# A front by contraction tiles, earlier splits for the last down tiles, and a step sooner at two changes of stage, in a one-core decoder-layer kernel

## The chip, the core and the metric

One core of a Trainium2 chip runs the whole layer in one launch. TensorE (PE) does the matmuls; VectorE (DVE), ScalarE (ACT) and GpSimd (POOL) work beside it, each with its own queue of instructions in order; SyncE (SP) issues most transfers. The metric is device time in microseconds (us) of one execution, the median over runs. One execution was recorded by the hardware profiler; its trace gives start and length of each instruction. Tiles are written partitions x columns.

## What is computed

520 tokens (a prompt of 512 and 8 decoding tokens of one step each), model width 1024, all in float32:

```python
def rmsnorm(x, g):
    return x * lax.rsqrt(jnp.mean(x * x, axis=-1, keepdims=True) + EPS) * g

def swiglu(x, w_gate, w_up, w_down):          # 1024 -> 2816 -> 1024
    return (jax.nn.silu(x @ w_gate) * (x @ w_up)) @ w_down

def layer(x, ...):
    x = x + 0.5 * rmsnorm(swiglu(rmsnorm(x, ffn1_pre_g), ...), ffn1_post_g)
    m, states = token_mixer(rmsnorm(x, mix_pre_g), ...)   # projections by w_in, retention and
    x = x + rmsnorm(m, mix_post_g)                        # gated DeltaNet, gates, w_out
    x = x + 0.5 * rmsnorm(swiglu(rmsnorm(x, ffn2_pre_g), ...), ffn2_post_g)
    return x, states
```

## The kernel before

**Products.** x is kept transposed: 8 contraction tiles (KD = 8) of 128 channels by 520 tokens, the tokens in two halves of 260 (HC). A float32 product is made of three passes in a reduced format (fp32r): each operand is split into hi, a cast on ACT, and lo, the rest, a subtraction on DVE; `passes` then issues hi·xh (L408), hi·xl (L409) and lo·xh (L410), all 128x260, into one bank of PSUM, of which there are 8. Weights are split by `split` (L350 cast `whi`, L351 subtraction `wlo`), x by `split_x` (L505 hi = x times the norm's gain, L506 lo; both in a tile `xhl`). The norm's factor 1/rms is per token and comes later, on what the product gives.

**Units and look-ahead.** The weights are a list of units in order of use (`units`): gate and up tiles 128x1024 of each ffn (`gu1`, `gu2`), down tiles in three pieces (8, 7 and 7 contraction tiles), mixer weights. The first PLAIN = 3 (ffn1) or 4 (ffn2) pairs of gate and up are plain products g and u; later pairs go by seven half-size products in place of eight (`sv` rows, from operands made by `token_factors`), as do most down tiles; the first and the last down tile (d = 0 and d = 7) are plain. `prefetch` loads and splits units up to `ahead` units before use (AHEAD = 2; 8 for the half-size ones), within SPLIT_BUFS = 9 buffers; a raw load goes out with two raw buffers.

**Tasks.** PE's order is the program's. Every few matmuls it calls `tick()`, which prefetches and steps small tasks (generators), each `yield n` waiting n ticks. The table LATER adds ticks to single steps by hand. So what an engine does between two other things is set by the tick in which it was written; an engine's queue then keeps that order.

**Front.** `load_first` loads unit 0 in four pieces of 128 KB, each followed by a 260 KB tile of the first token half of x, and then the second token half. `first_units` does g0 and u0, first for half 0 over all k, u0 after g0, then for half 1; the half-0 results are copied out of PSUM into `early`. POOL squares half 0 of x and sums it, ACT and DVE half 1; `inverse_rms` makes the sums over channels by small matmuls (`ss`, L471), the root on POOL, and spreads the factor over partitions by small matmuls (`rb`, L477), copied out by ACT (L559) and DVE (L557). 9 warm matmuls run before the first product.

**Changes of stage.** `down` makes y tile by tile with a sum of squares `acc`; the last tile, d = 7, is done by halves in `staged`. After each half `post` runs: `sums` (`ss`), `ms` on DVE and the root on POOL, `spread` (`rb`), and then for each k: t = y·rb (DVE, L629), x += t (POOL, L631), and two k later `split_x` of the new x. The next stage's products need these xhl. `post` also forces the split of the next stage's first units into that row. The new sum of squares (`pre_rms`) follows. At the very end `post_last` does the same without a next stage: for token half 1, six of the eight output tiles are added by PE (x by an identity product before, L586, t by another, L604, then a copy by ACT, L605, and a transfer of 130 KB each, L606), two by DVE (L608) with one transfer of 260 KB (L609).

Of the kernel before, what the change touches and what calls it, by code (L numbers as in the profile page):

```python
# [7 lines left out]
F32 = mybir.dt.float32  # L8
# [7 lines left out]
P = 128  # L16
# [19 lines left out]
TURN = 48  # L36
WARM = 9
RAW_BUFS, SPLIT_BUFS, AHEAD = 2, 9, 2
# [3 lines left out]
PLAIN = {1: 3, 2: 4}  # L42
SPLIT_H = (8, 21)


LATER = {
    ("begin", 0): {1: 1},
    ("decode_gdn", 0): {1: 8, 2: 2},
# [17 lines left out]
    ("gdn_head", 7): {0: 3},  # L66
    ("leads", 0): {1: 2},
    ("leads", 1): {0: 3},
    ("post", 0): {1: 2, 2: -1},
# [39 lines left out]
def units():  # L109

    out = []
    for f in (1, 2):
        for m in range(KF):
            if m < PLAIN[f]:
                out += [(f"gu{f}", 2 * m, 0, 8), (f"gu{f}", 2 * m + 1, 0, 8)]
# [55 lines left out]
class Kernel:  # L171
    def __init__(self, ctx, tc, a):
# [32 lines left out]
        self.sums_due = []  # L205
        self.hold_sums = True
        self.rooted = False
# [82 lines left out]

    def begin_pair(self, f, m):
# [8 lines left out]
        self.sums_due.append((self.now + SUM_LAG, g, s3, w[2 * m + 1, :, 0:KH]))  # L300
        self.sums_due.append((self.now + SUM_LAG, g, s1, w[2 * m + 1, :, KH:KD]))
        return s1, s3, a22
# [9 lines left out]
    def prefetch(self, force=False, most=9):  # L312
# [5 lines left out]
        while self.split_next < min(last, len(self.unit_list)):  # L318
            j = self.split_next
            seven = self.cost(j) == 1  # L320
            if self.unit_list[j][0] == "seven" and self.hold_sums and not force:
# [171 lines left out]

    def x_of(self, k, hf):
        return self.x[hf][k // 2][:, k % 2]

# [45 lines left out]

    def inverse_rms(self, acc, r, plus):
        nc = self.nc
# [5 lines left out]
        self.rooted = True  # L550
        self.hold = False
        yield 4
        out = self.wk.tile([P, TOK], F32, tag="rb", name=self.name("rb"), bufs=1)
        for hf, (c0, n) in enumerate(HALVES):
            pb = self.spread(s[:, hf * PIECES : (hf + 1) * PIECES])
            if hf:
                nc.vector.tensor_copy(out[:, c0 : c0 + n], pb)  # L557
            else:
                nc.scalar.copy(out[:, c0 : c0 + n], pb)  # L559
        for hf, (c0, n) in enumerate(HALVES):  # L560
            r[hf] = out[:, c0 : c0 + n]
        self.hold_sums = False

    def post_last(self, pairs, acc, sq, hf, plus):
# [28 lines left out]
        if hf:  # L593
            begin(KD - 2)
        for i in range(half):
# [17 lines left out]
    def post(self, y, acc, hf, gnext, xs, r, plus, plus_next):  # L613
# [4 lines left out]
        self.hold = self.hold_sums = True  # L618
        yield 2
        r2 = yield from self.rstd(acc, 1.0 / D, 3, plus and plus[0:PW, hf * PIECES : (hf + 1) * PIECES])  # L620
        if not hf:
# [4 lines left out]
        for k in range(KD + lag):  # L626
# [56 lines left out]
    def down(self, xin, pieces, gpost, gnext, held, plus=None, plus_next=None, x_from=None, seven=None):  # L683
# [39 lines left out]
        def load_x():  # L723
            self.x = self.x_tiles()
            for hf in range(2):
# [53 lines left out]

    def token_factors(self, xs, gcol, F, f):  # L780

        nc = self.nc
        while len(xs[1]) < KD or not self.rooted:
            yield 0

        for m in range(PLAIN[f], PLAIN[f] + 2):
            self.begun[f, m] = self.begin_pair(f, m)
        tt, stt = nc.vector.tensor_tensor, nc.vector.scalar_tensor_tensor
        for k in range(KH):
# [18 lines left out]
            F["B21"].append(xs[0][k + KH])  # L808
            F["B22"].append(xs[1][k + KH])
            yield 2  # L810

    def product7(self, table, F, name, banks, i):
# [14 lines left out]
    def ffn(self, plain, xs, r, gpre, gpost, gnext, plus, plus_next, x_from):  # L827
# [89 lines left out]

        self.spawn(self.token_factors(xs, gpre, F, 1 if x_from is self.a["xT"] else 2))
        lead = self.first_units(xs, "g", ((0,), (1,)) if x_from is self.a["xT"] else ((0, 1), (2, 3)))

        def leads():
            for j in range(0, len(lead), 2):
                yield from hidden(j // 2, *lead[j : j + 2])

        self.spawn(leads())
        for m in range(len(lead) // 2, plain):
            pg = self.product([(self.next_unit(), range(KD))], xs, "g")
# [57 lines left out]
    def run(self):  # L985
# [6 lines left out]
        nc.sync.dma_start(out=self.vec, in_=a["vec"])  # L992
        self.x = self.x_tiles()
        self.ones = c.tile([P, P], F32, name="ones")
# [5 lines left out]
        for i in range(WARM):  # L1000
            nc.tensor.matmul(ps[:, 0:P], self.ones, self.ones, start=True, stop=True)
        self.load_first()
        for k in range(0, KD, 2):
            nc.sync.dma_start(out=self.x[1][k // 2], in_=a["xT"][:, 1, k : k + 2])
        self.cst = c.tile([P, 3, P], F32, name="cst")
        nc.sync.dma_start(out=self.cst, in_=a["cst"])
        self.ident, self.triu, self.negm = (self.cst[:, i, :] for i in range(3))
        self.gh = c.tile([P, 16], F32, name="gh")
# [4 lines left out]
        xs, r = [[], []], [None, None]  # L1013
        for k in range(0, KD, 2):
            self.split(0, [slice(k, k + 2)])
            xs[0] += [self.split_x(k + z, 0, V_G1PRE) for z in range(2)]
        self.split(1, [slice(k, k + 2) for k in range(0, KD, 2)])
        xs[1] += [self.split_x(k, 1, V_G1PRE) for k in range(KD)]
        self.split(2, [slice(0, KD)])
        self.sq = [self.slot("sq") for _ in range(KD)]  # L1020
        for hf, (sq_eng, add_eng) in enumerate(((nc.gpsimd, nc.gpsimd), (nc.scalar, nc.vector))):
            c0, n = HALVES[hf]
            acc = self.sq[0][:, c0 : c0 + n]
            for k in range(KD):
                self.square(k, hf, sq_eng)
                if k:
                    add_eng.tensor_tensor(acc, acc, self.sq[k][:, c0 : c0 + n], ALU.add)
        self.ahead = AHEAD

        def begin():  # L1030
            yield 14
            yield from self.inverse_rms(self.sq[0], r, plus1)

        self.spawn(begin())
        xs, r = self.ffn(PLAIN[1], xs, r, V_G1PRE, self.gh[:, 0:8], V_MPRE, plus1, None, a["xT"])
# [16 lines left out]

    def load_first(self):

        nc, a = self.nc, self.a
        t = self.raw.tile([P, KD, P], F32, tag="raw", name=self.name("raw"))
        self.loaded[0] = t
        self.raw_next = 1
        for k in range(0, KD, 2):
            ks = slice(k, k + 2)  # L1060
            nc.sync.dma_start(out=t[:, ks], in_=a["gu1"][0, :, ks, :])
            nc.sync.dma_start(out=self.x[0][k // 2], in_=a["xT"][:, 0, k : k + 2])
        self.load_to(0)


    def evac_r(self, out, ps, r, off=0):
# [774 lines left out]
def layouts(i):  # L1841
    f = np.float32
    asc = np.ascontiguousarray
    out = {}
    x = np.concatenate([i["x_prompt"][0], i["x_sample"][:, 0]], 0)
    out["xT"] = asc(x.T.reshape(KD, P, 2, HC).transpose(1, 2, 0, 3))

# [3 lines left out]
    for n in (1, 2):  # L1851
        g, u = col_tiles(i[f"ffn{n}_w_gate"][0]), col_tiles(i[f"ffn{n}_w_up"][0])
        out[f"gu{n}"] = asc(np.stack([g, u], 1).reshape(2 * KF, P, KD, P))
        out[f"dn{n}"] = asc(col_tiles(i[f"ffn{n}_w_down"][0]))
    w = i["w_in"][0]
# [86 lines left out]
```

## Time and profile before

| | |
|---|---|
| median of 3 runs | 1201.34 us (1200.16 to 1201.74) |
| profiled execution | 1200.41 us, its span 1198.6 us, mean granted TensorE clock 0.996 |
| PE busy | 1179.1 us, 98% of the span |
| DVE, ACT, POOL busy | 913.7, 603.1, 273.5 us |
| moved by DMA | 170.90 MB, mean 143 GB/s |

The page gives busy time of each engine, the span in 40 slices, and groups of instructions by line; rows of the timeline are start, length, engine, line, operation, output<-inputs, shape, and in brackets the idle time before with what ended it. A row `PE g L409 <- DVE xhl L506: 4.1, 6, 1.0` says that PE waited 4.1 us in 6 waits, the longest 1.0, for DVE's line 506 to end. A matmul row's length overlaps the next one's start, so the pace of PE is read from starts.

### The profile page before, as it was taken

The numbers are of one execution on the slowest core, as the hardware profiler recorded it, in microseconds if no ns is written. First come the engines' busy times: TensorE is split into PE (matmuls) and PEld (weight loads), VectorE is DVE, ScalarE is ACT, GpSimd is POOL, SyncE is SP. The second block draws the span as 40 slices with busy tenths as digits, with TensorE's granted clock in tenths as the row PEclk, the third lists the DMA queues.
The fourth block names the chain that finished last, engine by engine and source line by source line (L and its number), as shares of the span: only waits on it lengthen the run. The fifth ranks groups of instructions, "written<-read, shape, count | busy, mean of one in ns | idle before, by whom it ended". The sixth has DMA issues, their size and how long they took to land. (4 is left out here: it accounts for less than half of the span.)

```text
span 1198.6 us, 25498 instructions
## 1 busy us (share of the span) xinstructions
PE 1179.1 (98%) x9835; PEld 1165.9 (97%) x9835; DVE 913.7 (76%) x1943; ACT 603.1 (50%) x1391; POOL 273.5 (23%) x492
## 2 busy tenths in 40 slices
PE   8999999999999999999999999999999999999998
PEld 8999999999999999999999999998999999999997
DVE  8988888777557788788677777746888888867554
ACT  6565666543336366323344774334555666644331
POOL 4211111000005148756451101404311111000000
PEclk8999999999999999999999999999999999999999
DMA  5877777132342343331467663242587777332342
GB/s 192 217 198 183 184 182 187 47 115 84 107 164 73 123 145 92 100 95 63 121 185 222 227 202 124 76 156 87 165 232 187 184 189 182 94 95 70 108 151 93
DMA packets 79034, 170.90 MB, mean 143 GB/s; under 512 B 17024, under 2 KB 18720, under 8 KB 78912
## 3 DMA queue, kind: packets, MB, share of 16 engines
q1 hardware_dynamic: 66624, 144.98, 37.6%
q0 software_dynamic: 12288, 24.29, 11.1%
q8 instruction: 77, 1.26, 0.4%
q14 instruction: 45, 0.37, 0.1%
HBM read 157.37 MB, written 11.86 MB: 141 GB/s over the span
## 5 line engine op out<-in xcount | busy, mean ns | idle before, releaser
L408 PE MATMUL p<-xhl,whi 128*128 128x260 f32 x784 | 231.0, 295 | 0.0
L409 PE MATMUL p<-xhl,whi 128*128 128x260 f32 x784 | 222.0, 283 | 1.4 <-DVE xhl L506 1.4
L410 PE MATMUL p<-xhl,wlo 128*128 128x260 f32 x784 | 221.4, 282 | 1.8 <-DVE wlo L351 1.8
L351 DVE TENSOR_TENSOR wlo<-raw,whi 128x1024 fp32r<-128x1024 f32 (+2 forms) x121 | 142.3, 1182 | 51.4 <-ACT whi L350 49.6
L408 PE MATMUL sv<-th,w 128*128 128x260 f32 x592 | 167.6, 283 | 0.5 <-ACT q L881 0.5
L409 PE MATMUL sv<-tl,w 128*128 128x260 f32 x592 | 167.6, 283 | 0.0
L410 PE MATMUL sv<-th,w 128*128 128x260 f32 x592 | 167.1, 282 | 0.0
L409 PEld LDWEIGHTS p<-xhl,whi 128*128 128x128 f32 x784 | 148.1, 189 | 2.0 <-DVE xhl L506 1.8
L410 PEld LDWEIGHTS p<-xhl,wlo 128*128 128x128 f32 x784 | 147.7, 188 | 2.2 <-DVE wlo L351 2.2
L408 PEld LDWEIGHTS p<-xhl,whi 128*128 128x128 f32 x784 | 147.9, 189 | 0.7
L350 ACT CAST whi<-raw 128x1024 fp32r<-128x1024 f32 (+2 forms) x121 | 116.3, 971 | 33.5 <-DMA raw<-dn_in 15.5
L369 DVE TENSOR_TENSOR w<-s,w 128x512 fp32r<-128x512 f32 x148 | 101.7, 689 | 37.9 <-ACT w L368 36.5
L307 POOL DMA_DIRECT2D s<-gu_in x74 | 65.1, 965 | 281.1 <-DMA s<-gu_in 93.6
L410 PE MATMUL dn<-hh,wlo 128*128 128x260 f32 x448 | 126.7, 283 | 1.2 <-DVE wlo L351 1.2
L408 PE MATMUL dn<-hh,whi 128*128 128x260 f32 x448 | 127.2, 284 | 0.1
L409 PE MATMUL dn<-hl,whi 128*128 128x260 f32 x448 | 126.7, 283 | 0.0
L410 PE MATMUL sv<-xhl,w 128*128 128x260 f32 x444 | 125.5, 283 | 0.0
L408 PE MATMUL sv<-xhl,w 128*128 128x260 f32 x444 | 125.5, 283 | 0.0
L409 PE MATMUL sv<-xhl,w 128*128 128x260 f32 x444 | 125.4, 282 | 0.0
L408 PEld LDWEIGHTS sv<-th,w 128*128 128x128 f32 x592 | 111.4, 188 | 0.9 <-ACT q L881 0.7
L410 PEld LDWEIGHTS sv<-th,w 128*128 128x128 f32 x592 | 111.8, 189 | 0.0
L409 PEld LDWEIGHTS sv<-tl,w 128*128 128x128 f32 x592 | 111.5, 188 | 0.0
(406 smaller groups left out, 3269.7 us busy)
## 6 DMA issues: line engine op xcount, KB each, us to landing
raw<-gu_in SPq DMA_DIRECT2D x50, 512.0 KB, 4.1
raw<-win_in SPq DMA_DIRECT2D x49, 512.0 KB, 3.6
s<-gu_in SPq DMA_DIRECT2D x74, 256.0 KB, 5.0
s<-gu_in POOLq DMA_DIRECT2D x74, 256.0 KB, 4.7
raw<-dn_in SPq DMA_DIRECT2D x32, 448.0 KB, 3.3
a<-gu_in SPq DMA_DIRECT2D x37, 256.0 KB, 5.0
x<-x SPq DMA_DIRECT2D x32, 260.0 KB, 5.1
raw<-dn_in SPq DMA_DIRECT2D x16, 512.0 KB, 3.5
```

Of the source, the lines that this page charges most:

```text
L307: self.nc.gpsimd.dma_start(out=out, in_=term, accum_op=ALU.add)
L350: self.nc.scalar.copy(hi[:, ks], t[:, ks])
L351: self.nc.vector.tensor_tensor(lo[:, ks], t[:, ks], hi[:, ks].bitcast(F32), ALU.subtract)
L369: nc.vector.tensor_tensor(w[:, 1], t[i], w[:, 0].bitcast(F32), ALU.subtract)
L408: mm(ps, hi[:, k, :], xh, start=first, stop=False, skip_group_check=more)
L409: mm(ps, hi[:, k, :], xl, start=False, stop=False, skip_group_check=more)
L410: mm(ps, lo[:, k, :], xh, start=False, stop=last, skip_group_check=more)
```

## The change

1. **Front.** The first three units (g0, u0, g1; LEAD = 3) are laid out by contraction tile (`lead`: 128 x 8 x 384) and x as `xk` (128 x 8 x 520), so that one load of 192 KB and one of 260 KB bring all that contraction tile k needs. `front` goes over k: for each, six banks (three units by two halves) get their 18 passes. ACT casts 384 columns of weights, scales 520 of x and squares 520; DVE subtracts twice and adds the squares up. POOL squares nothing any more, and the copies `early` fall away. The six loads of `begin_pairs` (first operands of the seven-product pairs) are issued right behind. WARM is 11. u1 is then done by halves (`staged`), with `ss` ahead of the last 18 passes of the front and `rb` with its two copies within u1.
2. **Last down tiles.** `prefetch` takes two units more of `ahead` for d = 7 of both ffns, so their three pieces are split earlier, and the third one's raw load goes out ahead of the x loads.
3. **Changes of stage** (`post`, first half). `sums` one tick sooner, `spread` one tick less behind; in `rstd` the next split is forced right behind `ms`, and in the row of k only where fewer than two units are split. Before the mixer this puts `ss` 6 matmuls sooner and `rb` 6; before ffn2 `ss` 6 sooner and `rb` 12.
4. **Tail.** Four output tiles by identity products in place of six; DVE adds the other four.

DVE at the front, before: `wlo` in quarters, xhl by halves of tokens (raw, x, vec: weights, activations and gains as loaded).

```order
L351 TENSOR_TENSOR wlo_130<-raw_107,whi_129 128x256
L506 SCALAR_TENSOR_TENSOR xhl_133<-x_85,vec,xhl_133 128x260
L506 SCALAR_TENSOR_TENSOR xhl_136<-x_85,vec,xhl_136 128x260
L351 TENSOR_TENSOR wlo_130<-raw_107,whi_129 128x256
L506 SCALAR_TENSOR_TENSOR xhl_141<-x_86,vec,xhl_141 128x260
L506 SCALAR_TENSOR_TENSOR xhl_144<-x_86,vec,xhl_144 128x260
L351 TENSOR_TENSOR wlo_130<-raw_107,whi_129 128x256
```

The same place now: per contraction tile the three units' lo, x's lo over all tokens, and from the third on the sum of squares.

```order
L1090 TENSOR_TENSOR wl_162<-leadw_101,wl_162 128x384
L1091 SCALAR_TENSOR_TENSOR xl_164<-x_103,vec,xh_163 128x520
L1090 TENSOR_TENSOR wl_169<-leadw_105,wl_169 128x384
L1091 SCALAR_TENSOR_TENSOR xl_171<-x_107,vec,xh_170 128x520
L1090 TENSOR_TENSOR wl_178<-leadw_109,wl_178 128x384
L1091 SCALAR_TENSOR_TENSOR xl_180<-x_111,vec,xh_179 128x520
L1103 TENSOR_TENSOR sq_176<-sq_176,sq_185 128x520
```

Two steps of DVE (a tile's lo of three units and of x) now carry 18 passes of PE; before, three steps (a quarter of `wlo`, two halves of tokens) carried 6. DVE at the end of ffn1, before (`wlo` 896 wide: the two seven-tile pieces of d = 7; `wlo_4821`, 1024: its third piece; `wlo_4827`: the mixer's first unit):

```order
L351 TENSOR_TENSOR wlo_4745<-raw_4467,whi_4744 128x896
L672 TENSOR_TENSOR c_4765<-dn_4750,u_4726 128x260
L653 TENSOR_TENSOR t_4767<-c_4765,dn_4564 128x260
L517 TENSOR_TENSOR acc_643_3486<-acc_643_3486,s_4770 128x260
L710 TENSOR_SCALAR y_4769<-t_4767,gh 128x260
L678 TENSOR_TENSOR v_4788<-q_4763,dn_4668 128x260
L653 TENSOR_TENSOR t_4790<-v_4788,dn_4565 128x260
L517 TENSOR_TENSOR acc_644_3487<-acc_644_3487,s_4792 128x260
L710 TENSOR_SCALAR y_4769<-t_4790,gh 128x260
L351 TENSOR_TENSOR wlo_4797<-raw_4630,whi_4796 128x896
L653 TENSOR_TENSOR t_4814<-u_4786,dn_4470 128x260
```

Now, same place:

```order
L351 TENSOR_TENSOR wlo_4678<-raw_4442,whi_4677 128x896
L351 TENSOR_TENSOR wlo_4726<-raw_4605,whi_4725 128x896
L682 TENSOR_TENSOR c_4746<-dn_4731,u_4707 128x260
L663 TENSOR_TENSOR t_4748<-c_4746,dn_4539 128x260
L523 TENSOR_TENSOR acc_649_3461<-acc_649_3461,s_4751 128x260
L720 TENSOR_SCALAR y_4750<-t_4748,gh 128x260
L351 TENSOR_TENSOR wlo_4756<-raw_4681,whi_4755 128x1024
L688 TENSOR_TENSOR v_4775<-q_4744,dn_4643 128x260
L663 TENSOR_TENSOR t_4777<-v_4775,dn_4540 128x260
```

The second piece stands eight steps sooner, the third ahead of two of the last evacuations instead of behind all. DVE at the change from ffn1 to the mixer, before:

```order
L463 SCALAR_TENSOR_TENSOR ms_4939<-ss_4935,plus_12_127 87x3
L629 TENSOR_TENSOR t_4959<-y_3710,rb_4955 128x260
L629 TENSOR_TENSOR t_4968<-y_3999,rb_4955 128x260
L351 TENSOR_TENSOR wlo_4972<-raw_4824,whi_4971 128x1024
L629 TENSOR_TENSOR t_4983<-y_4055,rb_4955 128x260
L506 SCALAR_TENSOR_TENSOR xhl_4986<-x_4728,vec,xhl_4986 128x260
```

And now:

```order
L463 SCALAR_TENSOR_TENSOR ms_4908<-ss_4904,plus_26_154 87x3
L351 TENSOR_TENSOR wlo_4919<-raw_4759,whi_4918 128x1024
L639 TENSOR_TENSOR t_4934<-y_3685,rb_4930 128x260
L639 TENSOR_TENSOR t_4943<-y_3974,rb_4930 128x260
L639 TENSOR_TENSOR t_4952<-y_4030,rb_4930 128x260
L512 SCALAR_TENSOR_TENSOR xhl_4955<-x_4709,vec,xhl_4955 128x260
```

The split moved out of the row of t. Before ffn2 a split of this kind keeps its place behind the second t.

The diff, cut:

```diff
-WARM = 9
+WARM = 11
+LEAD = 3
 LATER = {
-    ("begin", 0): {1: 1},
+    ("begin", 0): {2: 2},
...
 def prefetch(self, force=False, most=9):
             ahead += j > 0 and not seven and self.unit_list[j - 1][0] == "down7"
+            if self.unit_list[j][0][:2] == "dn" and self.unit_list[j][1] == KD - 1:
+                ahead += 2
...
-    def rstd(self, acc, scale, wait, plus):
+    def rstd(self, acc, scale, wait, plus, split=False):
         ps = self.bank("ss")
         self.sums(ps, acc, PIECES)
         _, r = self.root(ps, PIECES, scale, plus)
+        if split:
+            yield 1
+            self.prefetch(True, 1)
+            wait -= 1
         yield wait
         return self.spread(r)
...
 def post_last(...):
         if hf:
-            begin(KD - 2)
+            begin(KD // 2)
...
-            if hf and i < half - 1:
+            if hf and i < half // 2:
...
 def post(...):
-        yield 2
-        r2 = yield from self.rstd(acc, 1.0 / D, 3, ...)
+        yield 2 if hf else 1
+        r2 = yield from self.rstd(acc, 1.0 / D, 3 if hf else 2, ..., not hf)
...
-            if not hf and k == 1:
+            if not hf and k == 1 and self.split_next < self.use_next + 2:
                 self.prefetch(True, 1)
...
+        self.x, self.x_whole, self.lead_w = None, [], []
+        for k in range(KD):
+            self.lead_w.append(self.slot("leadw", (P, LEAD * P)))
+            nc.sync.dma_start(out=self.lead_w[k], in_=a["lead"][:, k])
+            self.x_whole.append(self.slot("x"))
+            nc.sync.dma_start(out=self.x_whole[k], in_=a["xk"][:, k])
+        self.load_to(0)
...
+    def front(self, xs, r):
...
+        def operands(k):
+            x, raw = self.x_whole[k], self.lead_w[k]
...
+            nc.scalar.copy(w[:, 0], raw)
+            nc.scalar.activation(hi, x, AF.Copy, scale=g)
+            tt(w[:, 1], raw, w[:, 0].bitcast(F32), ALU.subtract)
+            stt(out=lo, in0=x, scalar=g, in1=hi.bitcast(F32), op0=ALU.mult, op1=ALU.subtract)
...
+        for k in range(KD):
+            operands(k)
+            if k:
+                squares(k - 1)
+        squares(KD - 1)
...
+        for k in range(KD):
+            for j in range(LEAD):
+                for hf in range(2):
+                    self.passes(ws[k], j, xs[hf][k], banks[j][hf], k == 0, k == KD - 1)
+                self.tick()
+            self.release(1)
+            if k == KD - 3:
+                self.spawn(begin())
+                self.prefetch(True, 1)
```

More of the change, by code (lines that the diff above doesn't have):

```diff
@@ L112, in units @@
     for f in (1, 2):
-        for m in range(KF):
-            if m < PLAIN[f]:
-                out += [(f"gu{f}", 2 * m, 0, 8), (f"gu{f}", 2 * m + 1, 0, 8)]
+        out += [(f"gu{f}", j, 0, 8) for j in range(LEAD if f == 1 else 0, 2 * PLAIN[f])]
         out += [("seven", f, m, i) for m, i in stream(PLAIN[f])]
@@ L320, in prefetch @@
             seven = self.cost(j) == 1
-            if self.unit_list[j][0] == "seven" and self.hold_sums and not force:
+            if self.unit_list[j][0] == "seven" and (self.hold_sums or j >= self.pairs_upto) and not force:
                 break
@@ L809, in token_factors @@
             F["B22"].append(xs[1][k + KH])
+            if f == 1 and not k:
+                while not self.rooted:
+                    yield 0
+            elif f == 1 and k == 1:
+                while r[1] is None:
+                    yield 0
+                yield 2
+            elif f == 1 and k == KH - 2:
+                self.pairs_upto = 2 * PLAIN[1] - LEAD + 2
             yield 2
+        self.pairs_upto = len(self.unit_list)
     def product7(self, table, F, name, banks, i):
@@ L916, in pair, with up, leads @@
             return banks, at
[L918 to L926, printed above, removed]
+        self.spawn(self.token_factors(xs, r, gpre, F, 1 if x_from is self.a["xT"] else 2))
+        if x_from is self.a["xT"]:
+            lead = self.front(xs, r)
+            self.spawn(hidden(0, *lead[0:2]))
+            half = [None, None]
+            def up(j, hf, ps):
+                half[hf] = ps
+                if hf:
+                    self.spawn(hidden(1, lead[2], half))
+            self.staged([lambda: [(self.next_unit(), range(KD))]], KD, xs, "u", up, False)
+            done = 2
+        else:
+            lead = self.first_units(xs, "g", ((0, 1), (2, 3)))
+            def leads():
+                for j in range(0, len(lead), 2):
+                    yield from hidden(j // 2, *lead[j : j + 2])
+            self.spawn(leads())
+            done = 2
+        for m in range(done, plain):
             pg = self.product([(self.next_unit(), range(KD))], xs, "g")
@@ L1013, in run @@
         xs, r = [[], []], [None, None]
[L1014 to L1034, printed above, removed]
+        self.front_plus = plus1
         xs, r = self.ffn(PLAIN[1], xs, r, V_G1PRE, self.gh[:, 0:8], V_MPRE, plus1, None, a["xT"])
```

90 lines of the change are left out of this document (62 added, 28 removed).

## The prediction, before the run

> **What bounds the kernel now.** I read the page first, then TensorE's waits over the span, then a timeline and a table by stretch for the front, and last the places that the change touches. From the page, span, busy time and clock:
>
> ```profile
> span 1198.6 us, 25498 instructions
> ...
> PE 1179.1 (98%) x9835; PEld 1165.9 (97%) x9835; DVE 913.7 (76%) x1943; ACT 603.1 (50%) x1391; POOL 273.5 (23%) x492
> ...
> PEclk8999999999999999999999999999999999999999
> ```
>
> TensorE (PE) is busy 98% of the span, so only two things can move the time: matmuls that fall away, and time in which PE waits or runs below full clock. The clock is below full in the first slice alone. PE's waits over the whole span:
>
> ```profile
> PE g L409 <- DVE xhl L506: 4.1, 6, 1.0
> PE dn L410 <- DVE wlo L351: 2.0, 4, 0.6
> PE p L410 <- DVE wlo L351: 1.8, 2, 1.4
> PE p L409 <- DVE xhl L506: 1.4, 2, 1.0
> PE g L410 <- DVE wlo L351: 1.1, 2, 0.6
> PE u L408 <- ACT rb L559: 0.5, 1, 0.5
> PE u L408 <- DVE rb L557: 0.4, 1, 0.4
> ```
>
> Columns: total us, times, longest. Most rows lie where the change is made: the front (g on xhl), the two ends of a down stage (dn on wlo), the two changes of stage. The front, PE's rows one by one and then by stretch:
>
> ```profile
> 2.68 2.46 PE L1001 MATMUL warm<-ones 128*128 128x128 f32 x11
> 5.33 0.39 PE L408 MATMUL g<-xhl,whi 128*128 128x260 f32 x1 [0.19 <-ACT xhl L505]
> 6.29 0.39 PE L409 MATMUL g<-xhl,whi 128*128 128x260 f32 x1 [0.57 <-DVE xhl L506]
> 6.52 0.28 PE L410 MATMUL g<-xhl,wlo 128*128 128x260 f32 x1
> ...
> 9.19 0.42 PE L410 MATMUL g<-xhl,wlo 128*128 128x260 f32 x1
> 9.40 0.42 PE L408 MATMUL g<-xhl,whi 128*128 128x260 f32 x1
> ```
>
> ```profile
> 4.92:8.34 3.42, 1.87 (x9) 1.05 (x8) 3.03 (x4) 2.54 (x7) 3.26 (x5) 1.00 0.88 279
> 8.34:18.57 10.23, 8.52 (x33) 7.66 (x34) 10.23 (x16) 8.67 (x23) 7.96 (x11) 0.50 0.65 231
> 18.57:50.56 31.99, 31.99 (x274) 31.99 (x273) 29.87 (x60) 18.34 (x38) 7.06 (x7) 1.00 0.72 199
> 830.94:834.35 3.41, 2.27 (x17) 1.86 (x16) 2.43 (x3) 2.03 (x4) 0.33 (x1) 1.00 0.18 20
> ```
>
> Columns after the length: busy time of PE, weight loads, DVE, ACT, POOL, then granted clock, DMA share, GB/s. PE is starved in the first stretch (1.87 of 3.42 us), the clock then stands at 0.50 for 10.23 us, in which DVE is busy throughout, and only after that does PE run without a break. In the last row, a like thinning at the second change of stage, 2.27 us of work kept the clock. At half clock two starts lie 0.21 us apart (9.19, 9.40); at full clock three passes take 0.36, 0.12 each (next fence), and the row of 50.56 is the first `seven` product, the front's end. A wait costs more than its row says: the 0.57 before 6.29 stands for a start 0.96 after the last and one more of 0.23, 0.95 above two of 0.12. I add 0.3 for each wait below.
>
> ```profile
> 50.20 0.28 PE L408 MATMUL u<-xhl,whi 128*128 128x260 f32 x1
> ...
> 50.56 0.28 PE L408 MATMUL sv<-xhl,w 128*128 128x260 f32 x1
> ```
>
> **The front.** Six plain units of 48 matmuls are 6 x 48 x 0.12 = 34.6 us; the norm's `ss` and `rb`, 24 small ones, add 2.0 (31.99 less the other 250 x 0.12). So 36.6 us of work, which before took 50.56 - 5.33 = 45.2: 8.6 are lost. What the new order loses of that depends on its operands:
>
> ```profile
> 4.77 0.92 ACT L505 ACTIVATE xhl<-x,vec 128x260 fp32r<-128x260 f32 x2 [1.03 <-DMA x<-xT_in]
> ```
>
> ```profile
> 5.31 1.80 DVE L506 SCALAR_TENSOR_TENSOR xhl<-x,vec,xhl 128x260 fp32r<-128x260 f32 x2 [1.11 <-ACT xhl L505]
> ...
> 17.23 2.88 DVE L506 SCALAR_TENSOR_TENSOR xhl<-x,vec,xhl 128x260 fp32r<-128x260 f32 x7
> ```
>
> ```profile
> L351 DVE TENSOR_TENSOR wlo<-raw,whi 128x1024 fp32r<-128x1024 f32 x81 | 101.6, 1259 | 27.3 <-ACT whi L350 27.0
> L804 DVE TENSOR_TENSOR tl<-ta,th 128x520 fp32r<-128x520 f32 x8 | 5.5, 693 | 0.0
> ```
>
> ```profile
> L368 ACT CAST w<-s 128x512 fp32r<-128x512 f32 x148 | 91.3, 618 | 34.8 <-DVE s L364 23.8 <-PE sv L410 7.1 <-DVE s L372 3.4
> ```
>
> Transfers: a contraction tile is 192 + 260 KB, 0.46 MB. At the 279 and 231 GB/s of the first two stretches that is 1.7 to 2.0 us. The first x landed at 4.77 before, behind 128 KB of weights; now 64 KB more are ahead of it, 0.28 us: 5.05. DVE: the squares leave POOL, so the 0.90 us of a 128x260 subtraction (1.80 for two) becomes the 0.41 of the row at 17.23. A tile costs DVE a 384-wide subtraction (0.55, between 0.41 for 260 and 0.69 for 520), one of 520 and one addition of 520 (0.69 each): 1.9 us. ACT has three forms, 384 wide and twice 520, 0.62 at 512: 1.8. PE has 18 x 0.12 = 2.15. So PE is the slowest by a little, and all three hide behind it once it runs.
>
> It starts at 5.05 + 0.62 (ACT) + 0.69 (DVE) + 0.1 for handing over (before, ACT's first half ended at 5.23, PE began at 5.33) = 6.45. The warm rows ended at 5.14; two warm matmuls more, two rows each, end them near 5.6, so the window from 4.92 to 8.34 holds 0.7 us of them and about 16 passes of 0.12, some 2.6 us of work against 1.87: above the 2.27 that kept the clock. I take full clock throughout. Losses left: 6.45 - 5.33 = 1.1 at the start; 0.15 at the second tile (landed at 5.05 + 1.7 to 2.0, operands 1.3 later at 8.1 to 8.4, PE asking at 8.6; 0 to 0.3); 0.5 at u1's first third pass, whose split stands on DVE behind the last sums and the first token factors (8.4 + 6 tiles x 1.9 + a last addition 0.69 + four of 0.41 and two of 0.69 = 23.6, the split's end 1.26 later near 24.9), while PE asks near 24.4 (6.6 + 17.3, `ss`, two passes); 0.5 where `rb` and the second half of u1 take turns for banks that ACT and DVE must copy out (the `u` on `rb` rows, 0.5 and 0.4, are this hand-over in ffn2). Sum 2.2; end near 5.33 + 36.6 + 2.2 = 44.1. **-6.4**. Bounds: -7.5 (only the start lost), -4.7 (one more window at half clock, rival 1). The early `s` and `a` loads on SP stand behind all front loads; nothing of the front queues behind them.
>
> The Trainium skill ("DMA: Bandwidth & Descriptors", Measured) gives 138 GB/s for 64 KB, 341 for 1 MB, and asks for 1 MiB a transfer; reading 200 GB/s between them, an estimate, a tile takes 2.3 us and the front loses some 1.2 more. The stretches above, with transfers of 128 to 512 KB, ran at 231 to 279, so I keep those.
>
> **Last down tiles.** Two more units of lead put each `wlo` of d = 7 ahead of its use by up to two units more (21 matmuls, 2.5 us, each). What waits there now, at the end of ffn1 and of ffn2:
>
> ```profile
> PE dn L410 <- DVE wlo L351: 1.2, 2, 0.6
> ...
> PE dn L410 <- DVE wlo L351: 0.9, 2, 0.6
> ```
>
> 2.1 + 4 x 0.3 = 3.3; the last wait of the four, on a third unit whose load comes last, I count by half: **-3.0**; bounds -2.1 (the rows alone) and -3.5. The third unit's load goes ahead of x on SP; x is needed only after the sums, ten us on. The splits, up to 1.26 us each on DVE, go beside evacuations that PE doesn't wait for.
>
> **First change of stage.** Rows of the chain now (`rb` on PE, t on DVE, the next split's `wlo`, the first x operand):
>
> ```profile
> 363.67 0.80 PE L477 MATMUL rb<-cst,rs 87*128 87x87 f32 x6
> 364.51 0.76 DVE L629 TENSOR_TENSOR t<-y,rb 128x260 f32<-128x260 f32 x2 [2.02 <-PE rb L477]
> 365.19 1.71 DVE L351 TENSOR_TENSOR wlo<-raw,whi 128x1024 fp32r<-128x1024 f32 x1
> 365.85 0.51 ACT L505 ACTIVATE xhl<-x,vec 128x260 fp32r<-128x260 f32 x1 [5.17 <-POOL x L631]
> ```
>
> The first `lo` stands behind that `wlo`, and so does the third t. Now the sums come 6 matmuls sooner (0.72), and `wlo` stands between `ms` and the first t, in time that DVE spent idle ([2.02 <-PE rb]). PE's waits on p after it were 1.4 on xhl (two) and 0.4 on wlo (1.8 less its longest, which lies past 409 us and isn't touched): 2.7 with 0.3 for each. The chain is 0.72 earlier and 1.2 shorter (the 1.71 less what DVE would have waited for POOL in that time, 0.5): **-1.9**; bounds -0.7 (the earlier sums alone) and -2.7. New risk: `ss` comes before the accumulator is summed; it has 24 matmuls, 2.9 us, for ACT's square and DVE's addition, 0.46 + 0.41 by the rows above. Nothing.
>
> **Second change of stage.** Sums and `rb` 12 matmuls (1.44) sooner, but the `wlo` stays between two t:
>
> ```profile
> 819.81 1.66 DVE L351 TENSOR_TENSOR wlo<-raw,whi 128x1024 fp32r<-128x1024 f32 x1
> ```
>
> ```profile
> PE g L410 <- DVE wlo L351: 1.1, 2, 0.6
> PE g L409 <- DVE xhl L506: 1.0, 1, 1.0
> ```
>
> The wait on xhl (1.3 with its 0.3) goes. The two waits on the next splits stay: DVE has no less to do, and three evacuations (0.41 or so each) now stand inside the t row. `ss` follows the evacuation by 12 matmuls (1.4 us) where 0.46 + 0.41 are needed, behind whatever ACT and DVE are at (a 1024-wide split is 1.26): up to 0.7 of wait. **-1.2**; bounds -2.7 (all but one 0.3 of 2.1 + 0.9) and, if the evacuations (3 x 0.41) and that 0.7 exceed the 1.44, +0.5.
>
> **Tail.** Four output tiles by identity products:
>
> ```profile
> 1190.05 1.51 PE L586 MATMUL xo<-x,cst 128*128 128x260 f32 x6
> ...
> 1192.44 2.79 SPq L606 DMA_DIRECT2D yT_out<-x  x6
> ...
> 1195.32 0.40 SPq L609 DMA_DIRECT2D yT_out<-x  x1
> ```
>
> Two of the three x products after `rb` go (1.0 us), so the first t product starts when t is there, 0.45 sooner; SP has six issues of 0.47 in place of seven; DVE's one more addition of 520 (0.69) ends at about the same time. Last issue near 1194.5: **-0.7**; bounds 0 (the bytes decide) and -1.0.
>
> Sum: -6.4 - 3.0 - 1.9 - 1.2 - 0.7 = -13.2, from the profiled execution's 1200.41 to 1187.2. The median of the runs, 1201.34, lies 0.93 above that execution: 1188.1. All parts at their best give 1201.34 - 17.4 = 1183.9, all at their worst 1201.34 - 7.0 = 1194.3.
>
> **Rivals.** (1) One more window of 3.41 us at half clock, from 8.34: PE then does half, +1.7, 1189.8. For it: the clock fell here before; my 2.6 us of work is not far above 2.27, and operands 1 us late would put it below. The trace's fall came after a stretch with PE busy for 1.87 of 3.42 us. The Trainium skill ("TensorE: Matmul & The Clock Gate", Part 1: The HAM clock gate) has the clock fall only after an idle window, and its windows free-running; by that the front would keep its clock, as in my sum. A window more than half busy lost it here, so the trace doesn't bear that rule out; the phase no run here shows. (2) What the stage changes and down tiles gain is handed on: PE arrives sooner at splits that DVE does no sooner (the two `wlo` at the second change, the sums): 2 to 4 us of the 6.1 come back, 1191.1. For it: DVE is busy 76%. Against: waits later in both stages are small. (3) The other side: the front's operands come slower than PE. If a tile took p us instead of 2.15, the front would be 8 x (p - 2.15) longer; 13.2 us are used up at p = 3.8, where PE would also stand at half clock (18 x 0.21 = 3.8 a tile). Above it the kernel is slower: at 4.5, +5.6, 1207. There transfers would run at 0.46 MB / 4.5 us = 100 GB/s, or DVE at twice its rows. Against: 231 and 279. (4) The same at its edge: the front all at half clock, 3.8 a tile (+13.2), with the other gains kept: near 1201.3, no change. Against: 2.27 us of work in a window kept the clock, and DVE has 1.9 a tile.
>
> **How the numbers follow.** Forecast 0.68 (its own range 1185 to 1191), rival 1 0.14, rival 2 0.11, rival 3 0.03, rival 4 0.04. The range 1184.5 to 1192.5 holds the first three but for their edges. A measurement of this kernel tells 0.2%, 2.4 us, from no change: faster 0.93, same 0.04, slower 0.03.
>
> **What would show it.** Clock 1.00 after about 5 us and no 0.50 behind 8.34; the first sv near 44; `dn` on wlo gone from PE's waits; the waits of p on xhl gone, and no wlo between the t's at the first change; g on wlo still there at the second; new `u` on `rb` waits before 45 us; last output issue 0.7 us nearer to `rb`. A half-clock window in the front, or g waiting on transfers at each tile, would make it wrong.

## The result: 8.7 us faster, where 13.2 were forecast

| | before | after |
|---|---|---|
| median | 1201.54 us (4 runs, 1200.16 to 1202.13) | 1192.87 us (4 runs, 1192.46 to 1193.32) |
| profiled execution, its span | 1200.41, 1198.6 us | 1193.21, 1191.4 us |

The ratio is 0.9927, 95% interval 0.9911 to 0.9942. Forecast were 1188.1 and a range from 1184.5 to 1192.5. The page after, and PE's waits over the span (total us, times, longest):

```profile
span 1191.4 us, 25448 instructions
...
PE 1174.1 (99%) x9831; PEld 1163.2 (98%) x9831; DVE 907.3 (76%) x1935; ACT 602.9 (51%) x1378; POOL 262.4 (22%) x477
```

```profile
PE rb L477 <- POOL rs L465: 1.8, 3, 0.9
PE pV L1687 <- DVE pack L1679: 1.8, 2, 1.4
PE sv L408 <- ACT q L905: 1.8, 2, 1.2
PE p L410 <- DVE wlo L351: 1.4, 1, 1.4
```

The 4.1 us of g on xhl, the 2.0 of dn on wlo and the 1.4 of p on xhl are gone. Three of these four rows are new or larger: `rb` on POOL's root, pV (a step of the mixer's triangular solves) on DVE, and sv on ACT's copy q. The front, by rows and by stretch (length; busy time of PE, weight loads, DVE, ACT, POOL; granted clock; DMA share; GB/s):

```profile
5.90 0.39 PE L408 MATMUL g<-xh,wl 128*128 128x260 f32 x1
6.70 0.39 PE L409 MATMUL g<-xl,wl 128*128 128x260 f32 x1 [0.41 <-DVE xl L1091]
...
44.33 0.28 PE L408 MATMUL sv<-xh,w 128*128 128x260 f32 x1
```

```profile
5.61:9.02 3.41, 3.00 (x23) 2.62 (x22) 2.26 (x4) 2.68 (x6) 0.00 (x0) 1.00 0.98 328
9.02:44.33 35.31, 34.79 (x295) 34.61 (x294) 32.43 (x61) 24.75 (x47) 7.03 (x7) 1.00 0.84 238
640.49:643.90 3.41, 1.98 (x20) 1.73 (x19) 3.09 (x9) 0.64 (x2) 0.00 (x0) 1.00 1.06 328
643.90:647.32 3.42, 3.42 (x18) 3.42 (x17) 2.85 (x8) 1.57 (x9) 0.54 (x1) 0.50 0.96 331
```

The front went as forecast: first sv at 44.33 (forecast 44.1), full clock from 5.61, PE busy 34.79 of 35.31. The last row was not forecast: PE ran at half clock for 3.42 us in the mixer.

To see where time went, I cut each trace at the same matmuls of PE, counted from its first, and took the us between their starts. (With the front of before, four warm rows are fewer, and the count is four lower.) The last columns are kernels of the experiments below.

| stretch (rows of PE in the changed kernel) | before | after | front_only | no_front | after_again | ramp | split_before2 |
|---|---|---|---|---|---|---|---|
| front, to the first sv (334) | 50.56 | 44.33 | 44.71 | 51.06 | 44.49 | 44.14 | 44.56 |
| the next 46 | 5.48 | 7.29 | 7.26 | 5.48 | 7.26 | 5.52 | 7.27 |
| end of ffn1 (2830 to 2890) | 8.94 | 7.20 | 8.67 | 7.18 | 7.20 | 7.20 | 7.20 |
| first change (to 3060) | 23.09 | 22.51 | 23.05 | 22.57 | 22.53 | 22.52 | 21.91 |
| gates (3380 to 3420) | 4.70 | 4.72 | 6.24 | 4.68 | 6.23 | 4.71 | 4.72 |
| a solve (5340 to 5400) | 7.22 | 9.94 | 7.18 | 7.28 | 7.18 | 8.26 | 7.18 |
| second change (6750 to 6900) | 21.50 | 19.36 | 21.47 | 19.37 | 19.36 | 19.35 | 19.36 |
| end of ffn2 (9660 to 9710) | 7.74 | 6.00 | 7.47 | 6.01 | 6.00 | 6.00 | 6.00 |

So of the front's 6.2 us, 1.8 came back within 46 matmuls. The stretches repeat to 0.1 us between kernels that are alike there, but for the gates, the solve and the front's start. After minus before: -6.2 + 1.8 - 1.7 - 0.6 + 2.7 - 2.1 - 1.7 is -7.8; 1.3 more comes on in the long runs of products between, 0.9 of it from row 380 to 2830 (ffn1) and 0.4 in the mixer, and the tail has -0.6: -7.1, against 7.2 by the spans. Of the 0.9, 0.6 can't be put down to the change: no_front has it too, from row 1500 to 2830, where none of its edits acts yet.

### The profile page after: what moved, and what is told of

The parts are those of the page before. It is cut to its first block, busy times and chain, and to the rows that moved or that the text cites. A ratio compares the mean times of both kernels' runs of the same rounds, so it can differ in the third digit from the quotient of the medians.

```text
span 1191.4 us, 25448 instructions
## 1 busy us (share of the span) xinstructions
PE 1174.1 (99%) x9831; PEld 1163.2 (98%) x9831; DVE 907.3 (76%) x1935; ACT 602.9 (51%) x1378; POOL 262.4 (22%) x477
## 5 line engine op out<-in xcount | busy, mean ns | idle before, releaser
L351 DVE TENSOR_TENSOR wlo<-raw,whi 128x1024 fp32r<-128x1024 f32 (+1 forms) x111 | 133.0, 1203 | 50.0 <-ACT whi L350 48.4
L350 ACT CAST whi<-raw 128x1024 fp32r<-128x1024 f32 (+1 forms) x111 | 111.6, 1012 | 31.5 <-DMA raw<-dn_in 16.6
L368 ACT CAST w<-s 128x512 fp32r<-128x512 f32 x148 | 91.4, 618 | 33.8 <-DVE s L364 23.6
L465 POOL TENSOR_TENSOR rs<-ms,mhalf 87x3 f32<-87x3 f32 (+1 forms) x9 | 11.6, 1288 | 372.0 <-DVE ms L463 309.7
L410 PEld LDWEIGHTS dn<-hh,wlo 128*128 128x128 f32 x448 | 84.4, 188 | 0.0
```

Of the source, the lines that this page charges most:

```text
L350: self.nc.scalar.copy(hi[:, ks], t[:, ks])
L351: self.nc.vector.tensor_tensor(lo[:, ks], t[:, ks], hi[:, ks].bitcast(F32), ALU.subtract)
L368: nc.scalar.copy(w[:, 0], t[i])
L410: mm(ps, lo[:, k, :], xh, start=False, stop=last, skip_group_check=more)
L465: self.nc.gpsimd.tensor_tensor(r[0:PW], m[0:PW], self.mhalf[0:PW].to_broadcast([PW, n]), ALU.pow)
```

## The experiments

My theory after the result: the front's gain is handed on to splits behind it (theory 1), the first change loses to POOL's root, and the mixer's loss is an accident of the clock. The rivals are in the expectations.

**Parts alone or undone.** front_only: the first part without the others. no_front: the others without it. no_stage: `rstd`, `post` as before. no_down: without these lines:

```diff
-            if self.unit_list[j][0][:2] == "dn" and self.unit_list[j][1] == KD - 1:
-                ahead += 2
```

front_only:

> The new front alone; down tiles, changes of stage and tail as before. Theory 1 (the front's 6.2 us are partly handed on: PE meets the half-size splits before DVE has made them): first sv near 44.3, then a wait of 1.4 to 1.6 us on ACT's copy q near 49, some 3.6 us kept at the first dn tiles; in the mixer the wait on pack stays near 0.5 as before and the clock full: 3.4 to 4.0 us faster than before. Rival A (the front's own gain is all kept and the loss is due to the other parts): no wait near 49, 6 us faster. Rival B (whenever PE is some 5 us early in the mixer, the pack wait grows to 1.6 us and the clock falls for 3.4 us): as theory 1, but 1 to 1.5 us faster in all.

no_front:

> The front as before, with the earlier splits of the last down tiles, the sooner steps at both changes of stage and the short tail. Theory 1: the trace's differences hold one by one: 1.6 at the end of ffn1, 0.6 at the first change, 2.0 at the second, 1.6 at the end of ffn2, 0.7 in the tail, 6.5 us faster than before, with no loss of clock in the mixer. Rival A (the down and stage gains depend on the early front): below 4 us. Rival B (the pack wait and the lost clock come from the sooner steps, not from the front): 3.8 us, with the half-clock window near 650.

no_stage:

> The changed kernel with both changes of stage as before: sums, spread and the forced split at their old places. Theory 1 (at the first change the split right behind ms runs beside POOL's root and makes it 1.8 us in place of 0.9, and the second sums wait on DVE all the same, so that 0.6 us is all that was gained): root back at 0.9 us, the waits on xhl back to 1.4; the first change costs 0.6 more, the second 2.0 more: 2.6 us slower than the changed kernel unless the mixer's wait moves. Rival (the sooner steps gain what was forecast, 1.9 and 1.2): 3.1 us slower, and root at 0.9 in both.

no_down:

> The changed kernel without the two units more of lead for the last down tiles. Theory 1: waits of dn on wlo come back, two at each end, 1.6 us and 1.6 us: 3.2 us slower than the changed kernel if nothing else moves. Rival (the waits only move to the sums behind them, since DVE has no less to do): 1 us slower or less. The mixer's pack wait is a third reading of its size at another offset of PE: 1.6 again and a half-clock window if it depends on the new front, 0.5 if on PE being 5.5 us early.

Measured, against 1200.8 us of the kernel before on that chip (15 runs; the changed kernel was not run there, so what a part undone costs is read by stretch):

| | median us | ratio, 95% interval |
|---|---|---|
| front_only | 1198.42 | 0.9979, 0.9970 to 0.9988 |
| no_front | 1195.01 | 0.9950, 0.9936 to 0.9963 |
| no_stage | 1195.95 | 0.9957, 0.9944 to 0.9969 |
| no_down | 1194.93 | 0.9950, 0.9938 to 0.9963 |

The new front, worth 6 us at its end, is worth 2.4 in the whole (3.4 to 4.0 expected); the small edits are worth 5.8 (6.5 expected). By stretch the undone parts cost about what the changed kernel's trace had them gain: without the stage edits the first change takes 23.04 and the second 21.51 (0.5 and 2.2 more); without the down edit the two ends take 8.66 and 7.52 (1.5 each, for a gain of 1.7). Rival A of front_only falls: the wait near 49 is there with the front alone, and no_front has the 5.48 of before. The rivals of no_front and no_down fall as well: the small edits keep their gain without the new front, with no loss of clock near 650. My reading of the mixer held by half for front_only: the solve stayed at 7.18, so rival B falls too, but the clock was not full, since a window at half clock came elsewhere, at the gates. Busy time by stretch, and the gates' rows, of front_only:

```profile
415.72:419.13 3.41, 3.41 (x31) 3.36 (x30) 2.17 (x5) 3.41 (x12) 0.19 (x1) 1.00 1.04 391
419.13:422.55 3.42, 3.42 (x18) 3.42 (x17) 2.68 (x7) 2.60 (x14) 3.16 (x4) 0.50 0.59 178
```

```profile
415.83 0.29 PE L1335 MATMUL gc<-gg,cst 128*128 128x16 f32 x2
416.05 1.05 PE L1338 MATMUL gc<-cst,gg 8*128 8x8 f32 x8
416.97 1.03 PE L1338 MATMUL gc<-cst,beta 8*128 8x8 f32 x8
417.93 1.16 PE L1360 MATMUL gbc<-cst,gg 128*128 128x128 f32 x8
```

PE's rows fill the window from 415.72 (3.41 of 3.41), yet the clock fell behind it: 16 of its 31 matmuls were 8 columns wide on 8 partitions.

**The wait near 49.** What stands ahead of it in the changed kernel, on DVE, ACT and PE:

```profile
48.64 0.69 DVE L364 SCALAR_TENSOR_TENSOR s<-s,raw 128x512 f32<-128x512 f32 x1
```

```profile
49.36 0.62 ACT L368 CAST w<-s 128x512 fp32r<-128x512 f32 x1 [2.06 <-DVE s L364]
49.89 0.37 ACT L905 COPY q<-sv 128x260 f32<-128x260 f32 x1
```

```profile
50.31 0.39 PE L408 MATMUL sv<-th,w 128*128 128x260 f32 x1 [1.24 <-ACT q L905]
```

PE waits for a bank that ACT's copy q empties. The copy has long been possible (the last pass of its product starts at 47.09), but ACT first waits 2.06 us with a cast for DVE's sum s, of a unit that is needed some units later, and DVE is still at the splits of units up to 8 ahead. Counted in the traces, ACT had started 5 casts for half-size units by 2.5 us ahead of the first sv before the change, and 2 after it; in the next 5 us it starts 4 before, 7 after. Is it DVE's backlog from the front, or the order? no_sq_adds takes 4.8 us of additions off DVE (its norm is then another one, so it serves for the times alone); ahead5 keeps the work and shortens the look-ahead:

```diff
-            else:
-                tt(acc, acc, sq, ALU.add)
```

```diff
             ahead = 8 if seven and self.ahead else self.ahead
+            if seven and self.use_next < 2 * PLAIN[1] + 8:
+                ahead = 5
```

no_sq_adds:

> The changed kernel without the seven 128x520 additions of squares on DVE in the front (the norm's sum is then of the first contraction tile alone); all else as in the changed kernel. Theory D (DVE's backlog from the front, 4.8 us of it these additions, makes the half-size splits late): u1's wait on wlo is gone, and the 1.4 us before the sv product near 49 fall below 0.3, so 1.3 to 1.6 us faster than the changed kernel, first sv near 44.2 as there. Theory O (the copy q of a bank stands on ACT behind a cast that was split ahead of need, and the order alone makes the wait): the wait stays at 1 us or more.

ahead5:

> The changed kernel with the half-size units split at most 5 units ahead in place of 8 until the second pair of ffn1: the same work on DVE and ACT, in another order; copy q then stands behind no cast that waits for DVE's sum s2. Theory O (order): the wait near 49 falls from 1.4 to below 0.4 and no other of its size comes up in the next 10 us: 1.2 us faster than the changed kernel. Theory D (DVE's backlog): the wait goes over to w on DVE or to the next q, 1 us or more in all, and the time is the changed kernel's within 0.5 us.

no_sq_adds took 1191.64 us (0.9924, 0.9903 to 0.9945, against 1201.08) and has the wait unchanged; ahead5 took 1193.46 (0.9939, 0.9923 to 0.9956) and has it no more there, but has one where the look-ahead jumps from 5 to 8:

```profile
PE sv L408 <- ACT q L905: 1.2, 1, 1.2
```

```profile
68.40 0.36 PE L410 MATMUL sv<-xh,w 128*128 128x260 f32 x1 [1.81 <-ACT w L370]
```

(The first row: PE's waits of no_sq_adds from 44 to 75 us; the second: the timeline of ahead5.) So DVE's total isn't what makes the wait. In ahead5 it went over to the cast of an operand, not far from what theory D allowed, and behind it came a window at half clock (at 69.8), so that rows 380 to 1500 take 3.8 us longer than in after_again. Whether the burst makes the wait, or DVE has too little time in any order, was still open. To tell, ramp lets the look-ahead grow by one for every 14 units:

```diff
+            if seven:
+                ahead = min(ahead, 5 + max(0, self.use_next - 2 * PLAIN[1] + LEAD) // 14)
```

> The changed kernel with the half-size units split 5 ahead at first, and one more for every 14 units used, up to 8. Theory O (a burst of look-ahead splits, in the in-order queues of ACT and DVE, stands before the copies that free PE's banks; at a jump of the look-ahead from 5 to 8 the wait came back, 2.0 us): without a jump the wait near 49 is gone and none over 0.5 us comes before 100; 1.4 us faster than the changed kernel. Theory D (DVE has too little time for these splits in any order): a wait of 1 us or more comes later, no gain.

1190.99 us (0.9917, 0.9901 to 0.9932, against 1201.35). The 46 matmuls take 5.52 us, as before the change, ACT starts 5 of those casts in place of 7, and no wait comes from 44 to 75. Theory O holds by the stretch. By the median against the changed kernel's 1191.79 on the same chip, 0.8 us, it can't be told. Part of the 1.7 us is lost again later: rows 6900 to 8500, in ffn2, take 195.00 in place of after_again's 194.19, as they do in the other two kernels with a shorter look-ahead (195.01 in ahead5, 194.98 in ramp_split); why is open.

**The first change.** POOL's root, what DVE does beside it, and `rb`, in the changed kernel; and the root before:

```profile
356.59 1.81 POOL L465 TENSOR_TENSOR rs<-ms,mhalf 87x3 f32<-87x3 f32 x1 [148.43 <-DVE ms L463]
```

```profile
356.43 1.23 DVE L351 TENSOR_TENSOR wlo<-raw,whi 128x1024 fp32r<-128x1024 f32 x1
```

```profile
358.45 0.34 PE L477 MATMUL rb<-cst,rs 87*128 87x87 f32 x1 [0.59 <-POOL rs L465]
```

```profile
362.57 0.88 POOL L465 TENSOR_TENSOR rs<-ms,mhalf 87x3 f32<-87x3 f32 x1 [157.28 <-DVE ms L463]
```

The same root on 87x3 numbers takes 1.81 us in place of 0.88 when the wide subtraction runs beside it, and PE waits (in no_stage, without the split there, it takes 0.88 again). split_before_sums moved the split ahead of `ms`, but also put `rb` and the rest of `post` a tick sooner; split_before2 keeps all ticks:

```diff
+        if split:
+            self.prefetch(True, 1)
         ps = self.bank("ss")
         self.sums(ps, acc, PIECES)
         _, r = self.root(ps, PIECES, scale, plus)
         if split:
             yield 1
-            self.prefetch(True, 1)
             wait -= 1
```

split_before_sums (the same without `yield 1`):

> The changed kernel with the forced split at the first change of stage ahead of ms on DVE instead of right behind it. Theory R (a wide split on DVE beside POOL's root takes the root from 0.9 to 1.8 us, and rb waits for it): root back at 0.9, ms some 0.4 later, rb's wait at 357.6 from 0.9 to 0.4 or so, 0.4 to 0.5 us faster there. Rival (the root is long for another reason): root stays near 1.8 and rb's wait grows to 1.2. Its mixer tells again whether the pack wait of 1.6 us is there when the stages are sooner.

split_before2:

> The changed kernel with the forced split of the first change of stage ahead of ms on DVE, all other steps at their old ticks. Theory R (a wide split beside POOL's root makes the root 0.9 us longer and rb wait): root 0.9, rb's first wait at most 0.9 as it starts later by the split, x ready 0.5 sooner; the second ms and rb as in the changed kernel (wait 1.1 to 1.2); 0.3 to 0.6 us faster. Rival: the first operands of p aren't what the second ms waits for, so that rb 0.5 sooner only lengthens its wait: no gain within 0.2.

split_before_sums took 1196.52 us (0.9963, 0.9950 to 0.9975): the root was back at 0.88, but the tick put both next splits ahead of the second `ms` on DVE, and `rb` waited there for 3.7 us (first row, PE's waits from 340 to 380). split_before2 took 1190.54 (0.9909, 0.9896 to 0.9923, against 1201.35), with the first of the two waits gone (second row, waits from 354 to 380) and the root at 0.89:

```profile
PE rb L477 <- POOL rs L465: 4.4, 2, 3.7
```

```profile
PE rb L477 <- POOL rs L465: 0.9, 1, 0.9
```

```profile
357.40 0.89 POOL L465 TENSOR_TENSOR rs<-ms,mhalf 87x3 f32<-87x3 f32 x1 [148.99 <-DVE ms L463]
```

The stretch went from 22.5 to 21.91: 0.6 us, and the rival falls. The second wait, 0.9, stays. In the changed kernel `ms` stands there on DVE behind an x operand, and `rb` behind it on PE (before, `rb` didn't wait here):

```profile
368.55 0.49 DVE L512 SCALAR_TENSOR_TENSOR xhl<-x,vec,xhl 128x260 fp32r<-128x260 f32 x1 [0.29 <-ACT xhl L511]
368.96 0.15 DVE L463 SCALAR_TENSOR_TENSOR ms<-ss,plus 87x3 f32<-87x3 f32 x1
```

```profile
370.09 0.34 PE L477 MATMUL rb<-cst,rs 87*128 87x87 f32 x1 [0.92 <-POOL rs L465]
```

In split_before_sums it is this wait that grew.

**The mixer's solve.** solve_later puts the step that waits two ticks later (`yield 4` to `yield 6` ahead of pV64); after_again is the changed kernel once more.

> The changed kernel with the last step but one of each head's triangular solve (pV64) two ticks, 12 matmuls or 1.4 us, later in PE's order. Theory P (PE came 1.2 us too soon for a chain of small transfers, ACT and DVE, and the pause also cost the clock): the wait of 1.6 near 641 falls below 0.4, no half-clock window there, 1.2 to 2.8 us faster than the changed kernel. Rival (the head's chain is what is late, and PE waits at its next step instead): a wait of 1 us at pX or pu behind, and no gain.

> The changed kernel once more, on the chip of the next three. What is open: is the pack wait of 1.7 us at 641 a property of the kernel, or of one execution. If of one execution (it was 0.5 in three kernels that are the same there): 0.5 here, with a half-clock window elsewhere (near 417, in the stretch of the gates' small matmuls, or none). If of the kernel: 1.7 again and the half-clock window behind it. The sv wait near 49 (1.5) and rb's waits at the first change (0.9 and 1.2) are there again in both.

solve_later took 1195.37 us (0.9950, 0.9934 to 0.9966), so it gained nothing: its ratio is no better than the changed kernel's 0.9927 on another chip, waits of up to 1 us stand at the steps around, and rows 5400 to 6750 take 165.66 us where the changed kernel takes 163.06. after_again took 1191.79 (0.9917, 0.9904 to 0.9930); its solve waits 0.2 where the first trace waited 1.4, and its half-clock window lies at the gates (the waits of both from 636 to 646, first the changed kernel's first trace, then after_again's; then by stretch and the gates' rows of after_again):

```profile
PE pV L1687 <- DVE pack L1679: 1.4, 1, 1.4
```

```profile
PE pV L1687 <- DVE pack L1679: 0.2, 1, 0.2
```

```profile
413.74:417.15 3.41, 3.41 (x31) 3.36 (x30) 2.29 (x4) 3.41 (x13) 0.11 (x2) 1.00 1.04 395
417.15:420.57 3.42, 3.42 (x18) 3.42 (x18) 2.68 (x7) 2.59 (x12) 3.42 (x4) 0.50 0.55 176
```

```profile
413.63 0.29 PE L1341 MATMUL gc<-gg,cst 128*128 128x16 f32 x2
...
415.73 1.16 PE L1366 MATMUL gbc<-cst,gg 128*128 128x128 f32 x8
```

So both are of one execution, not of the kernel. Counted back from its window at 640.49 in steps of 3.413, the first trace had an edge at 415.2, in the middle of the same gate matmuls, and kept its clock there. The same count, from the first rise of the clock, can be made in all fourteen traces, and the half-clock windows behind the front start on its edges. The gates' 26 small matmuls last 3.0 us. In the four traces that lost the clock behind them (front_only, after_again, no_sq_adds, solve_later) one window held 2.9 to 3.0 us of them; in the ten that kept it, an edge divided them and the larger part was 1.7 to 2.7 us. The other three half-clock windows stand behind waits of PE of 1.4 us (the changed kernel's first trace), 1.8 (ahead5) and 3.7 (split_before_sums). The Trainium skill ("TensorE: Matmul & The Clock Gate", Part 1: The HAM clock gate) has windows of 3.4 us that run freely, so that the phase differs between runs; these traces agree. The solve's 1.2 us come from small transfers. In the first trace, DVE waits for them on the way to that pack:

```profile
633.60 0.31 DVE L1656 STREAM_TRANSPOSE pack<-pack 128x128 f32<-128x128 f32 x1 [1.17 <-DMA pack<-s]
```

The loads `pack<-s` were issued at 630.35, 8.8 us after the first of the eight stores `s<-pack` that they follow (621.55). In after_again it was 7.5 us (623.17 to 630.63), and DVE doesn't wait. no_down, ramp and ramp_split have the wait too (1.6, 1.0 and 1.2). Why these transfers took longer there stays open.

**Both edits.** ramp_split has ramp's and split_before2's:

> Both of the last two edits. If they are separate: the sum of their gains, 1.4 + 0.5, 1.9 us faster than the changed kernel, 1191 or less. If PE's lead is again handed on at the first change (DVE and POOL late there by as much as PE is early): only one of them counts, 1.0 to 1.4 us.

1191.29 us (0.9910, 0.9896 to 0.9924), its profiled execution 1190.17, the shortest of all. Both stretches have their gains (5.52 and 21.93), 2.3 us in the sum, but executions of one kernel on that chip differ by 2.7 to 4.5 us, the longest with a mean clock of 0.996 to 0.998, and the four medians on that chip (1191.79, 1190.99, 1190.54, 1191.29) can't be told apart. So these two edits are shown by stretch, not by time.

## Why the prediction was wrong

- **Front**: right in sum, -6.2 against -6.4, and in part by luck, since the terms differ more. The start and the first `lo` cost 1.4 (1.1 forecast), the second tile and u1's split less than 0.2 (0.15 and 0.5), the turns around `rb` 0.9 (0.5). (The working for u1's split adds up to 23.5, not 23.6.) The transfers ran at 328 GB/s in the window from 5.61, above my 231 to 279. The 1.2 us that my estimate from the Trainium skill ("DMA: Bandwidth & Descriptors", Measured) would have added did not come.
- **The step that failed first** is "Losses left" of the front: it followed DVE to u1's split and stopped there. The half-size units' splits, held back during the front (2 casts started in place of 5), then came in a burst (7 in place of 4), and ACT's in-order queue put a bank's copy behind them: +1.8. It is rival 2's kind (a gain handed on), at a place that I had not looked at, with a chance of 0.11.
- **First change**: -0.6 against -1.9. The step "in time that DVE spent idle" failed: DVE was idle, but POOL's root ran in that time, and beside a wide operation it takes 0.9 us longer; 0.6 of the missing 1.3 came back when the split was moved (split_before2). The other 0.7 I read from the trace only: the second `ms` stands on DVE behind an x operand, and `rb` waits 0.9.
- **Second change** -2.1 against -1.2, **down tiles** -3.5 against -3.0: right in kind, sized too small. Of the two waits of g on `wlo` that I left standing at the second change, one went (1.1 before, 0.5 after); the wait for `ss` that I feared was 0.4; and "Sums and `rb` 12 matmuls (1.44) sooner" is true of `rb` alone, the sums are 6 sooner. All four waits of dn went, and I had counted one by half. **Tail**: from row 9710 to the span's end 21.9 before, 21.3 after, -0.6 against -0.7.
- **"I take full clock throughout"** held in the front and failed behind it. A window at half clock costs 1.5 us at the gates (6.24 against 4.70), and seven of the twelve traces with the new front have one ahead of the tail (at 69.8, 373.8, 416 to 419 or 643.9). The three windows that the front of before lost were nearly free: of its 15 runs on the chip of the first four experiments, the three with a mean clock of 1.000 took 1200.32, 1200.44 and 1200.68 us, the five at 0.996, as three such windows give, 1200.38 to 1201.14 (where these five lost them was not recorded). It fits that DVE, busy 10.23 of 10.23 us in those windows of the trace, set the pace there, and not PE.

Together: 0.2 + 1.8 + 1.3 - 0.5 - 0.9 + 0.1 takes the forecast of -13.2 to -11.2. The solve (1.2) and one half-clock window (1.5) of the first trace make it -8.5, and the 1.3 in the long runs of products, which stay unexplained, -7.2, as that trace had. The medians, of executions with other windows, had -8.7 and, on another chip (after_again), -9.6.

## What to carry to other kernels

When a front gets faster, follow the in-order queues past its end: look-ahead work that was held back comes in a burst and stands before small copies that free a bank. Let a look-ahead grow step by step. Before work is moved into an engine's idle time, look at what runs on the other engines in that time: here a tiny step of POOL on the critical chain took twice as long beside a wide DVE subtraction.

## What the runs showed of the hardware

The clock fell after a window in which PE's rows were busy for 3.41 of 3.41 us, with 8x8 matmuls (419.13 in front_only, 417.15 in after_again), and it stayed full after one with 2.27 of 3.41 us of 128x260 passes (830.94 before). So the busy share of PE's rows isn't what the clock goes by, and whether the gates' small matmuls cost 1.5 us depends on where the windows' edges fall (2.9 us of them in one window lost the clock, 2.7 kept it). The rule that the prediction quoted from the Trainium skill ("TensorE: Matmul & The Clock Gate", Part 1: The HAM clock gate), that the clock falls after an idle window, doesn't fit these windows by the rows of the trace, and the measurement decides. The Trainium skill ("SBUF — State Buffer", Who interferes with whom) has a DVE operation with two inputs in SBUF contend with a GpSimd operation that reads SBUF; the root's 1.81 against 0.88 us beside the 128x1024 subtraction agrees.
